# The context stream's weight tiles are loaded through GpSimd's DMA queue while the experts run

## The chip, the cores and the metric

The kernel runs on one core of one Trainium2 chip. The metric is device time in microseconds (us) of one execution, as the median of several runs. The instruction streams of the core are those of TensorE (PE, with its weight loads PEld), VectorE (DVE), ScalarE (ACT), GpSimd (POOL) and SyncE (SP). SP computes nothing here: it issues DMA transfers. POOL and ACT issue some transfers too. Each stream runs in the order in which it is written, so an instruction that waits holds back everything behind it in its own stream.

## The reference

Two transformer blocks follow each other. The first is an AdaLN block with a state-space and attention mixer and a mixture of experts; the second has two layers over two streams, a latent of 512 tokens and a context of 256 tokens, at a width of 1024. Only the parts that matter here:

```python
# first block, after its mixer
h2 = rms_norm(x, norm2[layer]) * (1 + sc2) + sh2
moe_x = hier_moe(...)             # top-1 group of 4, top-2 of its 8 experts
x = x + g2 * moe_x
...
def expert_block(args):           # 32 experts, each (1024 x 512, 1024 x 512, 512 x 1024)
    xb, e = args
    return (jax.nn.silu(xb @ w_gate[e]) * (xb @ w_up[e])) @ w_down[e]
...
# second block, layer 0, context stream: needs nothing of the first block
hc = _modulate(xc, g_pre_mix[l], sc1, cc1)
kv_ctx = _kv_heads(hc @ w_in[l][:, :KV_COLS], k_norm[l])
xc = xc + gc1 * _rms_norm(_token_mixer(hc, kv_ctx, None, lp, lam, lam_init), g_post_mix[l])
hcm = _modulate(xc, g_pre_mlp[l], sc2, cc2)
xc = xc + gc2 * _rms_norm(_sq_relu_mlp(hcm, w_ff1[l], w_ff2[l]), g_post_mlp[l])
```

`_token_mixer` projects with `w_in`, runs four branches, multiplies each branch with its `w_br_*` and a gate, adds the four, and multiplies with `w_out`. `_sq_relu_mlp` is `square(relu(h @ w1)) @ w2` with a hidden width of 4096.

## The kernel before

The experts of the first block and layer 0 of the context stream are independent, and the kernel runs them side by side, in the stretch from about 555 to 1400 us. The program text is the context layer; the experts are a Python generator, `moe()`, which `dense` advances through `step` by a fixed pace (`PD` = 3.5 steps per dense block of 8 x 128 rows). So the two streams of work are woven into one order of instructions for each engine, and what comes out is that of a scheduler over both.

**Context.** A dense block multiplies a weight tile with the 256 context tokens in split precision. `wsplit` loads a tile W of 128 x 1024 floats (512 KB, `wload`, L254), ACT rounds it to its high part H (L263), DVE subtracts to get the low part (L264), and `mm3` makes three matmuls for each 128 rows: H by x high (L273), H by x low (L274), low by x high (L275). There are four W buffers and three H buffers. A W buffer is free again once DVE's subtraction has read it. The context's results go on to ACT: gates g (L1405), the hidden layer's relu t (L1732), rounding of the hidden layer Y (L294). The gated branches are summed on POOL (`u<-u,g`, L1412).

**Experts.** Tokens are sorted into 16 slot columns of 128 rows, worked through one after the other. For each, POOL gathers the rows xr by an indirect DMA (L1049), PE transposes them, and `two_experts` multiplies in groups of four We tiles of 512 KB (L1083, results `ex`), ACT does the activation ea (L1035) and copies the output ye (L1111), and POOL stores it to Y by a DMA (L1112). There are nine We buffers and two each of xr and ye. After slot column 11, one extra block of an expert with many tokens is computed; its We tiles come by 24 indirect DMAs that POOL issues (L1179), and its matmuls have line L1208. When the last expert is done, `moe()` goes on to a second part, `overflow` and `combine`.

**The queue.** All W and We tiles are loaded by the same line, L254, on SP, so in this stretch 108 loads of W stand among the experts' loads of We in one queue, in the order that the scheduler gave them. A load of We waits at the head of SP until the matmuls that last read its buffer are done. Eight loads of the context `xc` (L530) stand in SP's stream too, where the mixer's output projection begins.

Of the kernel before, what the change touches and what calls it, by code (L numbers as in the profile page):

```python
# [112 lines left out]
class Builder:  # L113
    def __init__(self, ctx, tc, io):
        self.tc, self.nc, self.io = tc, tc.nc, io
        self.med, self.bufs, self.alias = None, {}, {"sq": "t2"}
        self.beside, self.pace, self.due = iter(()), 0, 0
        self.ahead, self.ahead_med = None, None
        nc = self.nc
        pool = lambda name, bufs, **k: ctx.enter_context(tc.tile_pool(name=name, bufs=bufs, **k))  # L120
        self.cst = pool("cst", 1)
        self.small = pool("small", 2)
        work = pool("work", 2, reuse_waits="tile")
        sums = pool("sums", 1, space=bass.MemoryType.PSUM, reuse_waits="tile")
        self.bufs.update(W=(work, 4), H=(work, 3), t2=(work, 4), mm=(sums, 2), aux=(sums, 2))
        self.dram = pool("scr", 1, space=bass.MemoryType.DRAM)

        c = self.cst
        self.vec = c.tile([128, NV], F32, name="vec")
        nc.sync.dma_start(self.vec, io["vec"])  # L130
        self.con = c.tile([128, NCON], F32, name="con")
        nc.sync.dma_start(self.con, io["con"])
        self.ident = self.C("ident", 128)
        self.ones = {}
        t = c.tile([128, 4], F32, name="ones")
        for i, n in enumerate((1024, 512, 384, 128)):
            nc.vector.memset(t[:, i:i + 1], 1.0 / n)
            self.ones[n] = t[:, i:i + 1].to_broadcast([128, 32])
# [112 lines left out]

    def wload(self, flat, off, n, name="W", size=1024):
        t = self.new(name, [128, size])[:, :n]
        self.loaded = self.nc.sync.dma_start(t, bass.AP(tensor=flat.tensor, offset=flat.offset + off, ap=[[n, 128], [1, n]]))  # L254
        return t

    def wsplit(self, flat, off, k=8, width=128):
# [1525 lines left out]
def body(ctx, tc, io):  # L1783
    b = Builder(ctx, tc, io)
    nc = tc.nc
# [72 lines left out]
    def moe():  # L1858
        yield from b.experts(X, idx, p2, ends, sloti)
        inner.close()  # L1860
        with b.phase("p3", Wo=6, xr=1, xe=1, ye=1, ea=1, eh=2), b.banks("b3", ex=3, et=1):
            b.overflow(X, ends, nb)
        xpool.__enter__()
        x.extend(b.load_rows(xd, L, "x"))
        with b.phase("p4", yr=4, t2=4), b.banks("b4", aux=4):
            done.append((yield from b.combine(sloti, wt, x, b.V("norm_final", 0, 8))))
        yield
# [6 lines left out]
    b.alias["x256"] = "Y256"  # L1874
    b.med = cpool
    b.beside, b.pace = moe(), PD
    for i, _ in enumerate(b.rest):
        if i < 16:
            b.step(PA)
# [36 lines left out]
    for l in range(2):  # L1916
# [6 lines left out]
        if l == 0:  # L1923
            t = b.rows(4, L, "Q")
# [3 lines left out]
            t = b.rows(8, L, "Y", F32R)  # L1928
# [167 lines left out]
```

## Time and profile before

| what | before |
|---|---|
| time, median of 3 runs | 3632.12 us (3631.01 to 3633.67) |
| the profiled execution's own time | 3627.71 us |
| its span in the trace | 3625.9 us |
| granted TensorE clock, mean | 0.974 |
| PE busy | 3400.5 us (94%) |
| PE busy from 555 to 1400 us | 792.86 of 845.00 us |
| DMA share from 555 to 1400 us | 0.92, 339 GB/s |

The time is what counts; the span is what the trace covers of the profiled execution. The granted clock is a share of full speed (1.00 is the 2.4 GHz level). The DMA share is the mean busy share of the core's 16 DMA engines.

### The profile page before, as it was taken

How to read it: one execution, taken by the hardware profiler on the slowest of the kernel's cores; microseconds unless marked ns; L12 is line 12 of the kernel's file. 1: busy time of each engine (PE TensorE's matmuls, PEld its weight loads, DVE VectorE, ACT ScalarE, POOL GpSimd, SP SyncE). 2: the span in 40 equal slices, each digit the busy share in tenths (PEclk: the TensorE clock that was granted, in tenths of full speed). 3: DMA queues.
4: the chain of work that ended last, by engine and by line, in shares of the span. 5: the costliest groups of instructions: out<-in, count | busy, mean ns of one | idle time of the engine just before them, and what ended most of it. 6: DMA issues, size and time to landing. Idle time of an engine off the chain costs nothing. (4 is left out here: it accounts for less than half of the span.)

```text
span 3625.9 us, 50033 instructions
## 1 busy us (share of the span) xinstructions
PE 3400.5 (94%) x19244; PEld 2519.6 (69%) x19244; DVE 2024.5 (56%) x3987; ACT 1447.7 (40%) x2607; POOL 360.6 (10%) x350
## 2 busy tenths in 40 slices
PE   6998899999988998899999999999999999999998
PEld 3665477546555656777777877888677777878886
DVE  3665645664324434658877446444558887354444
ACT  3444334332223223446565334222356565233222
POOL 0003301101111200000000111000100010120000
PEclk7999899999999999999999999999999999999999
DMA  6567648999998997332211334323222211223331
GB/s 238 188 234 255 214 139 309 348 336 337 353 342 309 353 363 285 120 115 65 63 53 59 96 113 124 99 94 96 96 82 69 63 47 59 93 88 105 93 99 59
DMA packets 184897, 602.85 MB, mean 166 GB/s; under 512 B 21521, under 2 KB 34705, under 8 KB 184657
## 3 DMA queue, kind: packets, MB, share of 16 engines
q1 hardware_dynamic: 156672, 543.77, 43.4%
q0 software_dynamic: 15456, 36.98, 3.0%
q10 hardware_dynamic: 12528, 18.88, 1.5%
q8 instruction: 153, 2.51, 0.3%
q14 instruction: 88, 0.71, 0.1%
HBM read 570.44 MB, written 29.11 MB: 165 GB/s over the span
## 5 line engine op out<-in xcount | busy, mean ns | idle before, releaser
L273 PE MATMUL mm<-u,H 128*128 128x512 f32 (+1 forms) x2488 | 912.0, 367 | 38.7 <-ACT H L263 16.9
L275 PE MATMUL mm<-u,H 128*128 128x512 f32 (+1 forms) x2488 | 907.4, 365 | 8.0 <-DVE H L264 7.3
L274 PE MATMUL mm<-u,H 128*128 128x512 f32 (+1 forms) x2488 | 907.9, 365 | 0.5 <-DVE u L1692 0.2
L264 DVE TENSOR_TENSOR H<-W,H 128x1024 fp32r<-128x1024 f32 (+1 forms) x486 | 604.1, 1245 | 430.1 <-ACT H L263 428.9
L263 ACT CAST H<-W 128x1024 fp32r<-128x1024 f32 (+1 forms) x486 | 502.3, 1036 | 369.5 <-PE mm L275 228.5
L273 PEld LDWEIGHTS mm<-u,H 128*128 128x128 f32 x2488 | 472.5, 190 | 138.3 <-issue 33.0
L275 PEld LDWEIGHTS mm<-u,H 128*128 128x128 f32 x2488 | 471.6, 190 | 92.8 <-DVE H L264 13.5
L274 PEld LDWEIGHTS mm<-u,H 128*128 128x128 f32 x2488 | 472.8, 190 | 75.8 <-issue 8.8
L273 PE MATMUL mm<-Y,H 128*128 128x256 f32 (+1 forms) x792 | 271.4, 344 | 8.1 <-DVE u L1742 5.0
L274 PE MATMUL mm<-Y,H 128*128 128x256 f32 (+1 forms) x792 | 268.4, 339 | 0.4 <-DVE Y L295 0.4
L275 PE MATMUL mm<-Y,H 128*128 128x256 f32 (+1 forms) x792 | 265.8, 337 | 2.4 <-DVE H L264 2.4
L1083 PE MATMUL ex<-We,xe 128*64 128x512 f32 x1024 | 239.0, 609 | 3.0 <-DMA We<-in_wgu_dram 3.0
L1742 DVE TENSOR_TENSOR u<-u,mm 128x512 f32<-128x512 f32 (+1 forms) x168 | 100.5, 599 | 192.8 <-PE mm L275 192.5
L273 PEld LDWEIGHTS mm<-Y,H 128*128 128x128 f32 x792 | 150.8, 191 | 43.0 <-issue 12.5
L1733 DVE TENSOR_TENSOR t<-t,mm 128x512 f32<-128x512 f32 (+1 forms) x94 | 56.0, 596 | 218.3 <-ACT t L1732 218.3
L510 PE MATMUL sc<-KS,Q 128*128 128x256 f32 (+2 forms) x640 | 152.4, 352 | 23.9 <-ACT Q L500 15.6
L275 PEld LDWEIGHTS mm<-Y,H 128*128 128x128 f32 x792 | 150.5, 191 | 26.1 <-issue 7.5
L1732 ACT ACTIVATE t<-mm 128x512 f32<-128x512 f32 (+1 forms) x94 | 49.4, 526 | 297.8 <-PE mm L275 288.5
L274 PEld LDWEIGHTS mm<-Y,H 128*128 128x128 f32 x792 | 151.3, 191 | 19.2 <-issue 4.4
L1425 DVE SCALAR_TENSOR_TENSOR u<-pad,dw,u 128x512 f32<-128x512 f32 (+1 forms) x270 | 161.9, 656 | 0.2
L522 ACT COPY PT<-aux 128x512 f32<-128x512 f32 (+2 forms) x264 | 113.6, 473 | 116.8 <-PE aux L520 116.2
L1412 POOL TENSOR_TENSOR u<-u,g 128x512 f32<-128x512 f32 (+1 forms) x72 | 98.0, 1361 | 617.8 <-DVE g L1411 434.4
(548 smaller groups left out, 4796.2 us busy)
## 6 DMA issues: line engine op xcount, KB each, us to landing
We<-in_wgu_dram SPq DMA_DIRECT2D x256, 512.0 KB, 7.2
W<-in_win_dram SPq DMA_DIRECT2D x206, 512.0 KB, 3.7
W<-in_wff_dram SPq DMA_DIRECT2D x192, 512.0 KB, 3.6
We<-in_wdn_dram SPq DMA_DIRECT2D x128, 512.0 KB, 6.5
Wm<-in_wmod_dram SPq DMA_DIRECT2D x48, 512.0 KB, 4.7
W<-in_wmod_dram SPq DMA_DIRECT2D x48, 512.0 KB, 4.5
Wm<-in_wada_dram SPq DMA_DIRECT2D x32, 512.0 KB, 5.4
W<-in_wout_dram SPq DMA_DIRECT2D x32, 512.0 KB, 4.5
```

The source lines that it names most:

```text
L263: nc.scalar.copy(H, W)
L264: nc.vector.tensor_tensor(out=Lo, in0=W, in1=H.bitcast(F32), op=OP.subtract)
L273: self.nc.tensor.matmul(ps[:, :N], h, xh, start=start and k == 0, stop=False)
L274: self.nc.tensor.matmul(ps[:, :N], h, xl, start=False, stop=False)
L275: self.nc.tensor.matmul(ps[:, :N], l, xh, start=False, stop=stop and k == n - 1)
L510: self.nc.tensor.matmul(d, q[:, qs], k, start=i == 0, stop=i == 1)
L522: nc.scalar.copy(PT[:, a:a + n, :], src)
L1083: return lambda: self.nc.tensor.matmul(ps[64 * s:64 * s + 64], x(k, s), W[k - k0][:, s * 512:(s + 1) * 512], start=k == 0, stop=k == n - 1)
L1412: nc.gpsimd.tensor_tensor(out=mg[f], in0=mg[f], in1=g, op=OP.add)
L1425: t = nc.vector.scalar_tensor_tensor(y, pads[i][:, j:j + N], w, y, op0=OP.mult, op1=OP.add)
L1733: nc.vector.tensor_tensor(out=a, in0=a, in1=ps, op=OP.mult)
L1742: nc.vector.tensor_tensor(out=acc[f], in0=acc[f], in1=ps, op=OP.add)
```

## The change

The builder gets an attribute `wq`, the engine on whose queue `wload` puts tiles called "W". It is SP at first, is set to GpSimd where the experts' generator is made, and back to SP when the generator has yielded the last expert's work. Tiles called "We" stay on SP throughout.

```diff
@@ Builder.__init__
+        self.wq = tc.nc.sync
@@ wload
         t = self.new(name, [128, size])[:, :n]
-        self.loaded = self.nc.sync.dma_start(t, bass.AP(tensor=flat.tensor, ...))
+        queue = self.wq if name == "W" else self.nc.sync
+        self.loaded = queue.dma_start(t, bass.AP(tensor=flat.tensor, ...))
@@ body, moe()
         yield from b.experts(X, idx, p2, ends, sloti)
         inner.close()
+        b.wq = nc.sync
@@ body
     b.beside, b.pace = moe(), PD
+    b.wq = nc.gpsimd
     for i, _ in enumerate(b.rest):
```

In the changed program 105 loads of W stand in POOL's stream. Lines from the old L254 on carry numbers higher by two there.

**SP, in the context's MLP.** W is a tile of the MLP's `wff1` or `wff2`, We a tile of an expert's first two matrices (`wgu`) or its third (`wdn`). Before:

```order
L254 DMA W_12469<-in_wff1_dram 128x1024
L254 DMA We_12517<-in_wgu_dram 128x1024
L254 DMA We_12519<-in_wgu_dram 128x1024
L254 DMA We_12521<-in_wgu_dram 128x1024
L254 DMA W_12528<-in_wff2_dram 128x1024
L254 DMA We_12546<-in_wgu_dram 128x1024
L254 DMA We_12556<-in_wgu_dram 128x1024
L254 DMA We_12572<-in_wgu_dram 128x1024
L254 DMA We_12574<-in_wgu_dram 128x1024
```

The same place of SP's stream in the changed program:

```order
L256 DMA We_12452<-in_wdn_dram 128x1024
L256 DMA We_12517<-in_wgu_dram 128x1024
L256 DMA We_12519<-in_wgu_dram 128x1024
L256 DMA We_12521<-in_wgu_dram 128x1024
L256 DMA We_12546<-in_wgu_dram 128x1024
L256 DMA We_12556<-in_wgu_dram 128x1024
L256 DMA We_12572<-in_wgu_dram 128x1024
L256 DMA We_12574<-in_wgu_dram 128x1024
```

No W stands between the loads of We any more.

**POOL, in the context's branches.** The rows L1412 and L1414 are the sums of the gated branches, L1114 and L1112 a slot column's store of Y, L1051 and L1049 the gather of the next one's rows. Before:

```order
L1412 TENSOR_TENSOR u256_4864<-u256_4864,g_8347 128x256
L1412 TENSOR_TENSOR u256_4865<-u256_4865,g_8423 128x256
L1049 DMA xr_9257<-X_5463,idx16_5569 128x1024
L1112 DMA Y_2665<-ye_8417 128x1024
L1412 TENSOR_TENSOR u256_4866<-u256_4866,g_8495 128x256
```

In the changed program:

```order
L1414 TENSOR_TENSOR u256_4864<-u256_4864,g_8347 128x256
L256 DMA W_8669<-in_win2_dram 128x1024
L256 DMA W_8734<-in_win2_dram 128x1024
L1414 TENSOR_TENSOR u256_4865<-u256_4865,g_8423 128x256
L256 DMA W_8809<-in_wbr_dram 128x1024
L256 DMA W_8815<-in_win2_dram 128x1024
L1114 DMA Y_2665<-ye_8417 128x1024
L1051 DMA xr_9257<-X_5463,idx16_5569 128x1024
L1414 TENSOR_TENSOR u256_4866<-u256_4866,g_8495 128x256
```

The loads of W now stand between POOL's own work, each of which waits for DVE, ACT or PE; a load of W waits there for its buffer.

**ACT, in the context's MLP.** Rounding of the weights (H from W) among the context's and the experts' activations. Before:

```order
L263 CAST H_12416<-W_12414 128x1024
L1111 COPY ye_12352<-ex_12353 128x512
L1732 ACTIVATE t2_12462<-mm_12419 128x256
L294 CAST Y256_12412<-t2_12462 128x256
L263 CAST H_12471<-W_12469 128x1024
L1111 COPY ye_12352<-ex_12445 128x512
L1732 ACTIVATE t2_12523<-mm_12474 128x256
L263 CAST H_12530<-W_12528 128x1024
```

In the changed program:

```order
L265 CAST H_12471<-W_12469 128x1024
L296 CAST Y256_12297<-t2_12356 128x256
L1037 ACTIVATE ea_12343<-ex_12244 128x256
L1734 ACTIVATE t2_12407<-mm_12368 128x256
L265 CAST H_12530<-W_12528 128x1024
L296 CAST Y256_12361<-t2_12407 128x256
L1113 COPY ye_12352<-ex_12353 128x512
L1734 ACTIVATE t2_12462<-mm_12419 128x256
```

H_12530 stood behind the relu of mm_12474; it now stands ahead of that of mm_12419, two dense blocks earlier.

## Rows read from the trace of the kernel before

**Rows 1.** The page: busy time of each engine, share of the span, instructions.

```profile
PE 3400.5 (94%) x19244; PEld 2519.6 (69%) x19244; DVE 2024.5 (56%) x3987; ACT 1447.7 (40%) x2607; POOL 360.6 (10%) x350
```

**Rows 2.** Windows: length, busy PE, PEld, DVE, ACT, POOL; clock, DMA share, GB/s.

```profile
555.00:1400.00 845.00, 792.86 (x4870) 493.76 (x4869) 383.50 (x855) 256.22 (x509) 93.36 (x104) 0.99 0.92 339
1150.00:1250.00 100.00, 100.00 (x655) 69.27 (x651) 41.41 (x66) 32.77 (x58) 27.34 (x28) 1.00 0.89 324
1250.00:1300.00 50.00, 49.48 (x306) 30.68 (x306) 19.02 (x31) 12.06 (x19) 1.57 (x2) 1.00 1.01 388
1061.00:1069.00 8.00, 4.72 (x22) 4.36 (x22) 1.92 (x2) 1.04 (x1) 0.93 (x1) 0.57 1.03 368
```

**Rows 3.** Waits of PE, 555 to 1400: us in total, times, longest.

```profile
PE mm L273 <- ACT H L263: 11.5, 9, 2.8
PE aux L325 <- ACT t L343: 7.5, 7, 2.6
...
PE mm L275 <- DVE H L264: 5.0, 7, 1.5
...
PE ex L1083 <- DMA We<-in_wgu_dram: 3.0, 3, 1.6
...
PE cm L273 <- ACT H L263: 0.7, 2, 0.3
...
PE mm L273 <- DMA W<-in_wout_dram: 0.5, 1, 0.5
```

**Rows 4.** Tile W, 570 to 1390: who waited for it, issue to landing.

```profile
  ACT H L263: 46.8, 21
...
DMA to landing us min/median/max: 3.7/7.1/13.3
```

**Rows 5.** SP's timeline, 1282 to 1330: start, length, instruction, count.

```profile
1296.65 0.38 SPq L254 DMA_DIRECT2D W<-in_wff_dram  x1
1297.13 7.48 SPq L254 DMA_DIRECT2D We<-in_wgu_dram  x3
1304.70 1.34 SPq L254 DMA_DIRECT2D W<-in_wff_dram  x1
```

**Rows 6.** Timelines of DVE and ACT: the same buffer's release and its next rounding.

```profile
1288.57 1.22 DVE L264 TENSOR_TENSOR H<-W,H 128x1024 fp32r<-128x1024 f32 x1 [0.52 <-ACT H L263]
...
1311.46 1.04 ACT L263 CAST H<-W 128x1024 fp32r<-128x1024 f32 x1 [3.06 <-DMA W<-in_wff_dram]
```

**Rows 7.** Waits of SP, 555 to 1400: us in total, times, longest.

```profile
SPq L254 <- PE ex L1083: 491.6, 278, 11.8
```

**Rows 8.** Timelines of SP and PE, where the mixer's output projection begins.

```profile
1041.27 13.82 SPq L530 DMA_DIRECT2D xc<-in_ctx2T_dram x8
1055.67 0.38 SPq L254 DMA_DIRECT2D W<-in_wout_dram  x1
...
1063.88 0.58 PE L273 MATMUL mm<-u,H 128*128 128x256 f32 x1 [2.82 <-ACT H L263]
```

**Rows 9.** Waits of POOL, 555 to 1400: us in total, times, longest.

```profile
POOL u L1412 <- DVE g L1411: 211.2, 21, 38.2
POOL Y L1112 <- ACT ye L1111: 164.3, 9, 45.4
POOL xr L1049 <- PE et L1055: 144.1, 13, 44.5
...
POOL We L1179 <- PE ex L1083: 41.0, 5, 31.4
```

**Rows 10.** DMA, 555 to 1400: packets, MB, share by queue; issues' median landing.

```profile
q1 hardware_dynamic: 72710, 260.96, 83.4%
q0 software_dynamic: 8272, 24.39, 8.0%
...
We<-in_wgu_dram SPq DMA_DIRECT2D x256, 512.0 KB, 7.2
```

**Rows 11.** POOL's timeline: the first and last of the block's 24 loads, a store.

```profile
1166.35 0.99 POOL L1179 DMA_INDIRECT We<-in_wgu_dram,idx  x1 [31.43 <-PE ex L1083]
...
1207.16 0.95 POOL L1179 DMA_INDIRECT We<-in_wdn_dram,idx  x1 [0.30 <-issue]
...
1353.75 0.56 POOL L1112 DMA_DIRECT2D Y<-ye  x1 [45.44 <-ACT ye L1111]
```

More of the change, by code (lines that the diff above doesn't have):

```diff
@@ L253, in wload @@
         t = self.new(name, [128, size])[:, :n]
-        self.loaded = self.nc.sync.dma_start(t, bass.AP(tensor=flat.tensor, offset=flat.offset + off, ap=[[n, 128], [1, n]]))
+        queue = self.wq if name == "W" else self.nc.sync
+        self.loaded = queue.dma_start(t, bass.AP(tensor=flat.tensor, offset=flat.offset + off, ap=[[n, 128], [1, n]]))
         return t
```

## The prediction

> **What bounds the kernel now.** I began with the page's busy times: PE is busy for 94% of the span [rows 1], so the end moves only if PE works less, works at a higher clock, or waits less. The change takes no work from PE. It concerns the stretch in which the context and the experts share the core, so I cut the span by windows. From 555 to 1400 us PE is busy for 792.86 of 845.00 us [rows 2]: 52.1 us of idle time are all that a better order of loads can win there. The clock of this stretch is 0.99, with one dip that I come back to.
>
> The view of PE's waits says what those 52.1 us are [rows 3]. Four of its rows end with a context weight that was not ready: the matmuls of H waited for ACT's rounding (11.5 and 0.7 us), those of the low part for DVE's subtraction (5.0 us), one for a load itself (0.5 us). Together 17.7 us. The wait of the matmuls `ex` for We is only 3.0 us, and rows such as that of L325 on `t` L343 (7.5 us) are chains within norms and attention, without a weight in them.
>
> Next: why is H late? The view of tile W says that ACT sat idle for 46.8 us, 21 times, until a W had landed [rows 4], and that a load takes 3.7 to 13.3 us from issue to landing, 7.1 in the middle. SP's timeline shows why it was issued late [rows 5]: at 1296.65 a W goes out, then three We take 7.48 us, and only at 1304.70 comes the next W. The three We wait for matmuls of the experts (SP's wait on `ex` adds up to 491.6 us, 278 times [rows 7]), and W stands behind them. Was the W's own buffer free meanwhile? DVE's subtraction of four tiles earlier, which frees it, ran from 1288.57 for 1.22 us, so it was free at 1289.8; the load went out 14.9 us later, and ACT waited 3.06 us for it before it could start the rounding at 1311.46 [rows 6]. So the head of SP's queue, not the buffer and not the DMA engines, sets when this W comes. The longest case is where the output projection begins: SP spends 13.82 us on the `xc` loads, which wait for POOL's last sum, the W behind them goes out at 1055.67, and PE's first matmul of that projection waits 2.82 us [rows 8]. In the 8 us from 1061 to 1069 the granted clock is 0.57 [rows 2], close to the 1.2 GHz level, after that idle time of PE.
>
> **The change part by part.** It removes 105 loads of W from SP and adds 105 to POOL. Bytes, buffers and matmuls stay.
>
> (1) The waits for split weights. With its own queue, W can go out when its buffer is free, some 15 us before it did in the case above, where it was only 3.06 us too late. I take all 17.7 us as gone. Bounds: 0, if POOL's other work holds W back as long as SP did, and 17.7.
>
> (2) The clock. The dip costs 8.00 x (1 - 0.57) = 3.4 us of full-speed work. If the wait of 2.82 us ahead of it goes, the dip should go; but the neighbourhood has other short waits, so I count half: 1.7 us. Bounds 0 and 3.4.
>
> (3) SP without W. The loads of We run ahead a little more freely, but each still waits for `ex`; their total cost on PE was 3.0 us [rows 3]. I take 0, bounds a gain of 3.0 and a loss that is the first rival's.
>
> (4) POOL with W. POOL is busy for 93.36 of 845 us [rows 2], and a direct DMA occupies it 0.56 us [rows 11], so 105 more are 59 us: there is room. What matters is waiting. In POOL's order W stands behind sums that wait for DVE (longest 38.2 us), stores of Y that wait for ACT (45.4), gathers of xr that wait for PE's transposes (44.5), and indirect loads that wait for `ex` (31.4) [rows 9]. What counts is not how long those waits are, which mostly say that POOL had nothing to do, but whether the work waited for is done before W's buffer is free, or at most some 15 us after. The scheduler puts several W between one such row and the next, and each of these rows is needed by its own stream about when it comes. The place where it gets narrow is the extra block: 24 indirect loads of We between 1166.35 and 1207.16 [rows 11] now alternate with W. There W can be up to some 4 us late, but PE was busy for 100.00 of the 100 us around it [rows 2], so that other work covers a part. I take 2 us of loss; bounds 0 and 7.
>
> (5) POOL's own work behind W. A W that waits for its buffer holds back the sums, stores and gathers behind it, by up to a cycle of W buffers. xr and ye have two buffers for slot columns that are about 45 us apart (as the wait of 45.44 us for the store at 1353.75 shows [rows 11]), so a delay of 15 to 30 us stays inside that. The sums have two buffers g; a delay of up to 15 us stays just inside it. I take 0; the bounds lie in the second rival.
>
> (6) ACT's order. The rounding of a weight stands up to two dense blocks earlier among ACT's work. Where its W has landed and its H buffer is free it costs nothing; where H is not free, ACT's activations wait behind it. Before, ACT waited mostly for W and not for H, so 0 in the middle; the loss is bounded by what (1) gives.
>
> The sum: -17.7 - 1.7 + 2 = -17.4 us on the profiled execution, 3627.7 to 3610.3 us. The median of the runs before stands 4.4 us above the profiled one, and I add that: 3614.7, so **3615 us**.
>
> **A rule of the Trainium skill.** The rows show that POOL's queue moved 24.39 MB in 8.0% of the stretch and SP's 260.96 MB in 83.4% [rows 10]: 361 and 370 GB/s, so I see no slower path for W. The Trainium skill, "DMA: Bandwidth & Descriptors", section "SWDGE vs HWDGE vs iDMA", warns that the path of GpSimd is generally the slower one, and that its descriptors are written in memory from which DVE can lock GpSimd out. By that W would land somewhat later than 7.1 us after issue; no run here shows by how much, and the sum goes by the rows.
>
> **The rivals.** *No change.* The DMA engines are the real limit: their share is 0.92 on average and reaches 1.01 at 388 GB/s [rows 2]. Then W that comes earlier only pushes We later, and the 17.7 us come back as waits of `ex` for We, whose loads take 7.2 us in the middle [rows 10]. For it: stretches at a share of 1. Against it: 339 GB/s x 845 us is 286 MB, which at 388 GB/s takes 738 us, so 107 us are spare, and PE waits for We for 3.0 us only. It gives 3632. The Trainium skill has a rule that points the same way ("DMA: Bandwidth & Descriptors", "Issuing engines are not separate DMA queues"): whoever issues, transfers run on the same 16 engines, and a second issuer saves only the time of issuing. By that rule alone 105 issues would come off SP, which is not the engine that sets the end. My forecast rests on something else, the waiting in order ahead of the issue.
>
> *Slower: POOL's queue holds W back more than SP's did.* Each of the 16 slot columns has one store and one gather on POOL, and behind one of them a W comes too late. If PE then waits in each column as long as in its longest case of now, 2.8 us, that is 45 us; the 17.7 go, 45 come, 27 us net: 3659. For it: POOL's waits of 31 to 45 us [rows 9] are longer than SP's longest of 11.8 [rows 7]. Against it: their length is idle time, and W has about 15 us in hand. It decides from the point at which the row ahead of W on POOL comes more than those 15 us after W's buffer is free. Had two or three columns the fault, it would only eat a part of the gain.
>
> *More than forecast.* The waits inside norms and for We shrink too, since ACT no longer stands before a weight (46.8 us of its time): with the whole of (2), the 3.0 us of We and the 7.5 us of `t`, 17.7 + 3.4 + 3.0 + 7.5 = 31.6 us less: about 3600.
>
> **How the numbers follow.** A difference under about 0.2%, 7.3 us, is what a measurement of this kernel can't tell from no change. Chances: the forecast, anything from 8 to 24 us faster, 0.55; more than that 0.13; no change 0.17; slower 0.15. So faster 0.68, same 0.17, slower 0.15. The range reaches from the larger gain, 3600, to the lower part of the slower rival, 3642: it leaves out some 0.1 above and a few hundredths below. For the forecast alone it is 3608 to 3624.
>
> **What would show it.** Right: from 555 to 1400 the waits of PE for H from ACT and DVE fall from 17.2 to a few us; ACT's 46.8 us on W nearly vanish; W appears on POOL's timeline 10 us and more before its rounding; PE keeps its busy 793 us in a stretch some 17 us shorter; there is no dip near 1062; We still lands in about 7 us. Wrong: the waits of `ex` for We rise by 10 us or more with a landing well above 7.2 (first rival); POOL's loads of W follow directly on a late store, gather or indirect load, and ACT or PE wait for W right behind (second rival); or ACT's `t` and `g` come late behind a rounding that waits for H. What would make me wrong above all is the order on POOL: I infer from times of before when each row of it will be ready, and every delay there shifts the rows it was inferred from.

## The result: 1.2% faster, more than forecast

The changed kernel takes 3590.43 us (3584.6 to 3591.08), the kernel before 3632.89 us in the same runs; the ratio is 0.9876 with an interval of 0.9864 to 0.9887. That is 42.5 us less, where 17 were forecast and 3600 was the lower end of the range.

Where the time went can be read from one stretch in which both kernels execute the same work: from the last matmul of the routing to the last transpose of the experts' combined rows (`yr`). PE has 5279 matmuls in it in both. The windows view, before (length, busy time of PE, PEld, DVE, ACT and POOL, clock, DMA share, GB/s):

```profile
558.70:1461.50 902.80, 838.81 (x5279) 536.16 (x5280) 415.03 (x895) 279.84 (x543) 101.57 (x113) 0.98 0.90 333
```

And after:

```profile
555.90:1420.30 864.40, 825.69 (x5279) 533.91 (x5280) 411.82 (x895) 278.44 (x543) 156.24 (x218) 0.99 0.93 347
```

The stretch is 38.4 us shorter. PE's idle time falls from 64.0 to 38.7 us, by 25.3, and its busy time by 13.1. Of the busy time a part is clock: summed over windows of 10 us from 550 us on, (1 - granted clock) x 10 is 17.1 us before and 11.9 after. The rest of the two profiled executions differs by 4.7 us (3625.9 - 3582.8 = 43.1 us of span), 2.8 of it ahead of this stretch, which the change doesn't touch: PE's order there is the same in both.

The waits of PE in this stretch, after (us in total, times, longest), answer to [rows 3]:

```profile
PE ex L1085 <- DMA We<-in_wgu_dram: 10.2, 8, 3.6
PE mm L275 <- DVE t L1735: 6.0, 1, 6.0
...
PE ex L1085 <- DMA We<-in_wdn_dram: 1.2, 1, 1.2
...
PE aux L522 <- DVE P L1506: 0.9, 3, 0.4
...
PE cm L275 <- ACT H L265: 0.7, 2, 0.3
```

The waits for split weights have gone from 17.7 to 0.7 us. Waits for We have grown from 3.0 to 11.4. And waits that have no weight in them went too: that of L325 on `t`, 7.5 us before, has no row any more, and the wait of L522 on the attention's `P` is 0.9 us. Before, in the same view from 558.7 to 1461.5 us, that one stood at 5.5 us:

```profile
PE aux L520 <- DVE P L1504: 5.5, 7, 2.1
```

The view of tile W, after, answers to [rows 4]:

```profile
L256 POOL DMA_DIRECT2D W<-in_wff_dram x43: 530/530/600, 1044.2 to 1323.8; - x43
...
  POOL W L256: 352.5, 76
...
  ACT H L265: 0.2, 1
```

ACT waits for a W for 0.2 us in place of 46.8. It is POOL now that waits for DVE to free a buffer, 352.5 us at 76 of the 105 loads. Set against the end of the subtraction that frees the buffer, 93 of the 105 loads go out within 1 us of it, and 11 more than 3 us after it (30.3 us at most).

### The profile page after: what moved, and what is told of

It reads as the page before. It is cut to its first block, busy times and chain, and to the rows that moved or that the text cites. A ratio compares the mean times of both kernels' runs of the same rounds, so it can differ in the third digit from the quotient of the medians.

```text
span 3582.8 us, 50037 instructions
## 1 busy us (share of the span) xinstructions
PE 3382.2 (94%) x19244; PEld 2514.2 (70%) x19244; DVE 2020.7 (56%) x3987; ACT 1446.2 (40%) x2607; POOL 414.3 (12%) x455
## 5 line engine op out<-in xcount | busy, mean ns | idle before, releaser
L275 PE MATMUL mm<-Y,H 128*128 128x256 f32 (+1 forms) x792 | 272.0, 344 | 12.5 <-DVE t L1735 6.0
L512 PE MATMUL sc<-KS,Q 128*128 128x256 f32 (+2 forms) x640 | 151.2, 349 | 24.5 <-ACT Q L502 15.7
L1085 PEld LDWEIGHTS ex<-We,xe 128*64 128x64 f32 x1024 | 70.1, 138 | 130.9 <-issue 118.4
```

The costliest lines, as they stand in the source:

```text
L275: self.nc.tensor.matmul(ps[:, :N], h, xh, start=start and k == 0, stop=False)
L512: self.nc.tensor.matmul(d, q[:, qs], k, start=i == 0, stop=i == 1)
L1085: return lambda: self.nc.tensor.matmul(ps[64 * s:64 * s + 64], x(k, s), W[k - k0][:, s * 512:(s + 1) * 512], start=k == 0, stop=k == n - 1)
```

## The experiments

The changed kernel differs from the one before in two things at once, and the order rows ahead of the prediction show both: the queue on which W is loaded, and the order in which the scheduler then wrote the instructions of PE, ACT and DVE. The first two experiments take them apart. `hold_order` runs at the end of the kernel's text; it ties each instruction of an engine to the one that stood before it in the other kernel, so that the scheduler can only write that order. In the stretch, the rows of the engines that were held stand in the traces in the order that was meant, by operation and tile.

```diff
+def hold_order(tc):
+    t = json.loads(zlib.decompress(base64.b85decode(ORDER)))
+    at = {i.name: i for i in tc.nc.cur_bb.bb.instructions}
+    info = mybir.DependencyInfo(mybir.DependencyClass.NoSync, mybir.DependencyReason.DATA)
+    for steps in t.values():
+        n, names = 0, []
+        for d in steps:
+            n += d
+            names.append(f"I-{n}")
+        names = [x for x in names if x in at]
+        for first, then in zip(names, names[1:]):
+            tc.add_manual_dep(at[then], first, info, reason="pace")
...
     inner.close()
     xpool.__exit__(None, None, None)
+    hold_order(tc)
```

**The new queue with the old order.** The changed kernel, with ORDER holding PE, ACT and DVE to the kernel before.

> W on GpSimd's queue as in the change, but PE, ACT and DVE held to the order of the kernel before. Theory 1 (the queue does it at run time: W lands before it is needed, whatever the order): within 8 us of the changed kernel, 3590. Theory 2 (two things: the queue takes away the 17 us of waits for split weights and a little clock, the scheduler's new order of PE, ACT and DVE takes away the waits in softmax and norms): 3608 to 3620, with the waits of PE for H gone and those of L1504's P and L343's t still there.

Measured: 3628.3 us against 3628.84, ratio 0.9997 (0.9988 to 1.0005): no change at all. Both theories said that the queue alone gives something. Its windows row, and its waits of PE (lines stand five higher than in the kernel before):

```profile
558.90:1464.50 905.60, 840.16 (x5280) 536.72 (x5280) 413.71 (x895) 277.63 (x543) 161.27 (x218) 0.98 0.91 332
```

```profile
PE mm L278 <- ACT H L268: 9.3, 9, 1.8
PE aux L330 <- ACT t L348: 7.5, 7, 2.6
PE mm L280 <- DVE H L269: 6.2, 7, 1.7
...
PE aux L525 <- DVE P L1509: 6.0, 7, 2.1
```

The waits for H are still there, although no row of ACT's waits names a load of W any more (46.8 us before). The timelines of POOL, ACT and PE show why, at the tile W_12528 of the order rows:

```profile
1333.68 0.53 POOL L259 DMA_DIRECT2D W<-in_wff_dram  x1 [3.77 <-DVE H L269]
...
1359.47 0.38 ACT L1737 ACTIVATE t<-mm 128x256 f32<-128x256 f32 x1 [2.58 <-PE mm L280]
1359.75 1.04 ACT L268 CAST H<-W 128x1024 fp32r<-128x1024 f32 x1
...
1360.84 0.39 PE L278 MATMUL mm<-Y,H 128*128 128x256 f32 x1 [1.08 <-ACT H L268]
```

W goes out 26 us before its rounding. But the rounding stands behind the relu `t` in ACT's order, which waits 2.58 us for PE's matmul, and PE then waits 1.08 us for the rounding. In the kernel before the same rows stand at 1356.04, 1356.32 and 1357.41, with the same 2.58 and 1.08 us:

```profile
1356.04 0.38 ACT L1732 ACTIVATE t<-mm 128x256 f32<-128x256 f32 x1 [2.58 <-PE mm L275]
1356.32 1.04 ACT L263 CAST H<-W 128x1024 fp32r<-128x1024 f32 x1
...
1357.41 0.38 PE L273 MATMUL mm<-Y,H 128*128 128x256 f32 x1 [1.08 <-ACT H L263]
```

So at this tile it was the place in ACT's order that made H late, and not the load: the rounding had no idle time for a load even in the kernel before. Taken wait by wait, PE waits 18 times for H in the kernel before, 17.2 us in all; only at 5 of them, 4.7 us, had ACT waited for the load ahead of the rounding. The other 13, 12.5 us, stand here at the same matmuls with the same lengths. What the early loads took away is the wait of 2.82 us where the output projection begins, and 1.7 us of that came back in waits behind it. The tile that the prediction took as its example, for which ACT waited 3.06 us, had cost PE 0.21 us, and costs 0.21 us here too:

```profile
1317.05 0.39 PE L275 MATMUL mm<-Y,H 128*128 128x256 f32 x1 [0.21 <-DVE H L264]
```

Over all 105 loads, the start of the rounding less the start of the issue in the timelines is 10.6 us in the middle before, 24.5 here and 22.5 in the changed kernel: here the weights are as early as there, and it gains nothing.

**The old queue with the new order.** The kernel before, with ORDER holding PE, ACT and DVE to the changed kernel.

> All loads on SyncE's queue as before, but PE, ACT and DVE held to the order of the changed kernel. Theory 1: about 3632, as before. Theory 2: the order alone gives the other part, 3608 to 3620. Rival to both: the order is only good with early weights; the roundings stand earlier in ACT's order, wait there for W, and hold back activations: 3640 and more.

Measured: 3673.59 us, ratio 1.0115 (1.0098 to 1.0131). The rival holds: this order is only good with early weights. From its waits, of ACT and then of PE:

```profile
ACT H L266 <- DMA W<-in_win_dram: 45.5, 6, 13.9
...
ACT H L266 <- DMA W<-in_wff_dram: 44.6, 7, 9.7
ACT H L266 <- DMA W<-in_wbr_dram: 21.8, 5, 6.9
ACT H L266 <- DMA W<-in_wout_dram: 12.6, 1, 12.6
```

```profile
PE et L1043 <- DVE ea L1040: 33.5, 7, 9.1
PE aux L1464 <- ACT PT L525: 11.8, 1, 11.8
PE mm L276 <- ACT u L300: 10.4, 1, 10.4
```

ACT stands 124.5 us at roundings whose W has not landed, and PE waits for what is queued behind them on ACT and DVE, the experts' activation `ea` above all. Neither half gains; together they give 42 us.

**Other queues.** First the two queues exchanged, We on GpSimd's and W on SyncE's; then W on ACT's queue. The scheduler is free in both.

```diff
-        queue = self.wq if name == "W" else self.nc.sync
+        queue = self.eq if name == "We" else self.nc.sync
```

> The queues exchanged: the experts' We on GpSimd's queue, W alone on SyncE's. If the separation is what counts: 3585 to 3600. If it counts that the stream with 9 buffers and the sharper need stays clear of POOL's waits: PE waits for We behind stores, gathers and sums, 3640 or more.

```diff
-    b.wq = nc.gpsimd
+    b.wq = nc.scalar
```

> W on ACT's DMA queue. If any second queue does it: 3585 to 3600. If a load that waits for its buffer holds back the work behind it on its engine: ACT, which computes for the path, stands behind each load that waits, and part or all of the gain is lost: 3600 to 3650.

Measured: 3600.33 us, ratio 0.9919 (0.9904 to 0.9933), and 3587.54 us, ratio 0.988 (0.9863 to 0.9897). So it need not be POOL that issues, and it need not be W that moves, though We on POOL's queue gives only two thirds of the gain. PE's waits for We add up to 15.6 us there, against 11.4 after the change; these 4.2 us are half of the 8.5 us by which its stretch is longer. Whether POOL's stores, gathers and sums cause them, or the order that the scheduler wrote for this kernel, is not shown. They do not bring 3640. ACT, which computes for the path, loses nothing visible by issuing W. By the timeline its stream stood 88 times at a load whose buffer was not free yet, but for 3.6 us at most.

**PE's order alone, ACT's order alone.** The changed kernel, once with PE alone and once with ACT alone held to the order of the kernel before; the scheduler is free on the other engines.

> W on GpSimd's queue; PE alone held to the order of the kernel before, ACT and DVE free, so the scheduler may put the roundings early. Theory A (early W counts through early roundings in ACT's and DVE's order): most of the gain, 3588 to 3602. Theory B (it counts through PE's own order, which puts experts' matmuls where softmax and norms wait): little or none, 3612 to 3630.

> W on GpSimd's queue; ACT alone held to the order of the kernel before, PE and DVE free. Theory A: little or nothing is gained, 3615 to 3635, and PE waits for H as before. Theory B: most of the gain, 3588 to 3605.

Measured: 3618.99 us, ratio 0.9969 (0.9955 to 0.9982), and 3620.9 us, ratio 0.9972 (0.9959 to 0.9984). Each gives a quarter of the gain. The first lies in the range of theory B, the second in that of theory A: neither order does it alone, and both theories, as one cause each, fall. With PE held, ACT may round early, and PE's waits for H fall from 17.2 to 1.4 us; but the waits on `t` and `P` are as long as before:

```profile
PE aux L330 <- ACT t L348: 10.3, 8, 1.7
...
PE aux L525 <- DVE P L1509: 5.2, 6, 2.1
```

With ACT held, a part of the waits for H stays, and PE waits more for We:

```profile
PE ex L1088 <- DMA We<-in_wgu_dram: 17.9, 11, 4.3
...
PE mm L278 <- ACT H L268: 4.2, 4, 1.3
PE aux L330 <- ACT t L348: 3.5, 3, 1.6
```

Without either of the two orders most of the gain is missing. How it divides between them these runs don't show, since an order made for one kernel and held in another can cost something by itself (the waits for We here); DVE's order was never held alone.

**One queue, in the right order.** If the order is what counts, a second queue should not be needed. The kernel before, all loads on SyncE, with PE, ACT and DVE held to the changed kernel, and SyncE's loads held to the order in time in which the changed kernel's two queues issued theirs.

> All loads on SyncE's one queue, in the order in time in which the changed kernel's two queues issued them; PE, ACT and DVE in the changed kernel's order. If the order of the loads among each other is what the second queue buys: 3585 to 3605. If one queue is not enough, since a load that waits for its buffer holds back the other stream: 3610 to 3640, with waits of PE for We or of ACT for W.

Measured: 3585.85 us, ratio 0.9872 (0.9857 to 0.9887): the whole gain, on the one queue that the kernel before had. From its windows and its waits of PE and ACT:

```profile
559.30:1421.10 861.80, 825.59 (x5279) 533.89 (x5280) 411.58 (x895) 278.13 (x543) 97.36 (x113) 0.99 0.93 349
```

```profile
PE ex L1086 <- DMA We<-in_wgu_dram: 11.7, 9, 4.6
...
ACT H L266 <- DMA W<-in_wff_dram: 2.8, 1, 2.8
ACT H L266 <- DMA W<-in_win_dram: 1.8, 1, 1.8
```

It differs from the second experiment, which is some 88 us slower, only in where W stands among the loads of SyncE (and in one load of We that goes ahead of `xc` in place of behind it): PE, ACT, DVE and POOL have the same order in both traces. A load that waits there for its buffer holds back the other stream without a cost that shows.

Then the same order of SyncE's loads, with PE, ACT, DVE and POOL left to the scheduler.

> All loads on SyncE's one queue, held there to the order in time in which the changed kernel's two queues issued them; PE, ACT, DVE and POOL left to the scheduler. If what the change did was to let the scheduler see the weights early, so that it writes the better order by itself: 3583 to 3597. If the order that it writes for one queue is another one: 3605 to 3632.

Measured: 3613.42 us, ratio 0.9958 (0.9945 to 0.9972), a third of the gain, as the second expectation had it. Given the loads in this order on one queue, the scheduler wrote another order for the engines than it did for two queues, with roundings that are late again (PE waits 5.1 us for H behind ACT and 3.2 behind DVE, and a W goes out only 13.4 us in the middle ahead of its rounding).

**Where in the stretch.** The change in the mixer only, then from the output projection on only.

```diff
+    b.wq = nc.sync
     xc = b.load_x("ctx2T", LC, "xc")
```

> W on GpSimd's queue only until the mixer's output projection begins, on SyncE's in the projection and the MLP. In the trace of the changed kernel the experts' extra block begins 33 us earlier than before, and the experts end 38 us earlier. If the gain lies in the mixer: 3595 to 3608. If by the waits for split weights, most of which lie after 1000 us: 3612 to 3625.

```diff
-    b.wq = nc.gpsimd
     for i, _ in enumerate(b.rest):
...
+    b.wq = nc.gpsimd
     xc = b.load_x("ctx2T", LC, "xc")
```

> W on GpSimd's queue only from the mixer's output projection on. If the two parts add up (the mixer alone gave 0.8% of 1.2%): 3612 to 3622. If the gain of the second part hangs on the first: 3626 to 3636.

Measured: 3603.19 us, ratio 0.9921 (0.9907 to 0.9934), and 3612.68 us, ratio 0.9963 (0.9951 to 0.9974). 0.79% and 0.37% make 1.16 of 1.24%: the two parts add up, and two thirds lie in the mixer, where PE had the fewer waits for split weights (7.3 of 17.7 us, ahead of 1041 us).

**Three W buffers.** The changed kernel with `W=(work, 3)` in place of 4, in the whole program.

> The changed kernel with three W buffers in place of four, in the whole program. A load can then be issued one dense block later at the earliest. If W has some 10 us and more in hand behind GpSimd's queue: 3588 to 3598. If the fourth buffer is what lets the loads be early: 3605 to 3640.

Measured: 3655.26 us, ratio 1.008 (1.0065 to 1.0095). Taken as a whole this speaks for the fourth buffer, but the windows row of the stretch doesn't:

```profile
614.30:1480.60 866.30, 826.48 (x5279) 535.09 (x5280) 412.99 (x896) 278.56 (x543) 156.67 (x218) 0.98 0.92 347
```

The stretch is 866.3 us long, 1.9 more than with four. It only begins at 614.3 in place of 555.9 us: the loss of 58 us lies ahead of it, in parts of the program that load W on SyncE as before. In the stretch itself a buffer less costs next to nothing: a W still goes out 17.2 us in the middle ahead of its rounding, against 22.5 with four.

## Why the prediction was wrong

The direction and the disappearance of the waits for split weights were right. The cause behind them was not, and so the size was not either. On the two profiled executions the waits for split weights gave 17.0 us, waits without a weight in them 16.7, PE's shorter busy time 13.1, the rest of the program 4.7, and We took 8.4: 43.1 us, where the sum had 17.4.

**The step that failed is part (1) together with part (6).** I read that a W landed 3.06 us after ACT was ready for it, and concluded that SP's head of queue "sets when this W comes", which is true, and that an earlier W takes the waits of PE away, which is not. With W 24.5 us ahead in the middle and the old order, the waits for H were 9.3 and 6.2 us in place of 11.5 and 5.0, and the time was the same. The roundings stood in ACT's order behind work that waits for PE, so PE made its own weights late. The trace of before had it already: I put ACT's 46.8 us on loads and PE's 17.2 us on H together without following one into the other, and only 4.7 of the 17.2 us came behind a rounding that had waited for its load. I had the rows of ACT's order ahead of the prediction, with roundings up to two dense blocks earlier, and put 0 beside them, with losses only as bounds. That move, with the loads early enough for it, was the change. The 17.7 us were the right number for the wrong reason: 17.0 went.

**What "no weight in them" left out.** I excluded the waits on `t` and `P` from the forecast, since no weight stands in those chains. Together with smaller ones they fell by more than 16 us (`t` 7.5 to none, `P` 5.5 to 0.9, the transposes of `ea` 3.5 to 1.5, and so on, in the views of PE's waits). With PE's order held they stayed; in the new one they went. PE's order differs in its weave of experts' and context's matmuls. For `t` its timeline shows what that does. Between the output projection and the MLP the norms have ten groups of sums on `t` before (L325, 1058 to 1133 us); five stand directly behind a group of experts' matmuls `ex`, and none of these waits, while four of the other five do (4.7 of the 7.5 us). After the change nine of eleven groups stand behind `ex` (1037 to 1110 us), and none waits. One of each, before and after:

```profile
1076.29 0.28 PE L275 MATMUL mm<-u,H 128*128 128x256 f32 x1
1077.47 0.41 PE L325 MATMUL aux<-t,ones 128*32 128x128 f32 x4 [0.91 <-ACT t L343]
```

```profile
1059.52 3.65 PE L1085 MATMUL ex<-We,xe 128*64 128x512 f32 x16
1063.11 0.41 PE L327 MATMUL aux<-t,ones 128*32 128x128 f32 x4
```

For `P` it is not as clear: three of its seven waits stood behind `ex`. My case "more than forecast" had 31.6 us with a chance of 0.13. It let `t` and the waits for We go because ACT would no longer stand before a weight; in the first experiment ACT no longer did, and `t` stayed at 7.5 us. It left out P and all of the clock but the one dip.

**The clock (2).** 1.7 us were counted for one dip, near 1062 us. By windows of 10 us the stretch had others, near 795, 975 and 1120 to 1140 us, and the sum of the loss fell by 5.2 us. That the dip goes with the wait ahead of it was right: in the first experiment the granted clock is 1.00 from 1060 to 1070 us. But dips came elsewhere there, near 565, 695 and 805 us, and the sum stayed at 17.1 us. Some 8 us of the 13.1 by which PE's busy time fell are not in the granted clock. What they are stays open.

**We (3).** Taken as 0, with a gain as the first bound; it was a loss of 8.4 us, 3.0 to 11.4. The stretch is shorter with the same bytes, at 347 in place of 333 GB/s, and the first rival was right that We pays for a part. In the first experiment, with W as early and the old order, those waits were 4.8 us, so most of the growth came with the new order; how much of it is the DMA engines' is not shown. It is a fifth of the gain and no limit: PE is busy for 10.00 of 10 us in most windows between 1180 and 1350 us after the change, where DMA stands at 353 to 414 GB/s.

**POOL, (4) and (5).** Right in that nothing on POOL held the path up: POOL's waits passed to W's buffers (352.5 us), and the views show no wait of PE for a rounding behind them. In the extra block W went out up to 5.1 us late, close to the 4 us expected, but no rounding waited for it, so the 2 us of loss were not seen. The slower rival, that POOL's queue holds W back more than SP's, is refuted by the first experiment, where W has a median lead of 24.5 us behind that queue.

**The page.** The first experiment's W took 3.8 to 19.0 us from issue to landing on POOL's queue, 7.2 in the middle, against 7.1 on SP's, so the slower path that the Trainium skill gives to GpSimd ("DMA: Bandwidth & Descriptors", "Issuing engine by pattern") does not show in a 512 KB load. Its other rule, in "Issuing engines are not separate DMA queues", is that a second issuer saves only the time of issuing. I set it aside with the argument that waiting in order is what is saved. One queue in the right order is as fast as two (ratios 0.9872 and 0.9876): the runs agree with the page. Of my argument a part holds: with the new order of the engines, W's place among SyncE's loads is worth 88 us. But with the old order it was worth nothing, and it takes no second queue.

Shown is: the order of PE, ACT and DVE, with loads early enough for it, makes the gain; the number of queues and the issuing engine do not. Argued, not shown, is why the scheduler writes that order when W has a queue of its own: it lays out the engines by its own idea of when a load arrives, which is earlier there. That it wrote another one for the same loads on one queue, held to the order of the changed kernel, fits this but doesn't prove it.

## What to carry to other kernels

Where a scheduler writes the instruction order, a change of queue is a change of every engine's order; look at what moved on the engines that compute before pricing the wait that the change is named after, and hold the order fixed once to see which of the two pays. A wait that ends with a load is not the load's fault if, with the load early, the same instruction would have waited for what stands ahead of it on its own engine: read the row before it, too, and follow it to the engine that bounds the kernel before you count it. And early weights and an order that uses them were worth nothing apart here: no change for the weights without the order, a loss of 1.2% for the order without the weights.

## What the runs showed of the hardware that was not expected

ACT's DMA queue carried 105 loads (101 of 512 KB, 4 of 384 KB) among ACT's own work without a cost that shows (ratio 0.988, beside 0.9876 on POOL's); that a load which waits for its buffer would hold back the activations behind it did not show, at waits of 3.6 us and less. And the DMA engines kept up 400 GB/s and more in many windows of 10 us (1.03 at 408 GB/s from 1210 to 1220 us after the change) while PE had no idle time: a DMA share of 1 over such windows was not what bound PE.
